# Far queries, far keys and four gate tiles by Strassen's scheme in a one-core decoder layer

## The chip, the core and the metric

The kernel runs on one NeuronCore of a Trainium2 chip. Five engines work side by side, each with its own instruction queue that is taken in order: PE (matrix multiply; its weight loads are shown as PEld), DVE (elementwise), ACT (elementwise and activation functions), POOL (here almost only an issuer of DMAs) and SP (an issuer of DMAs). Semaphores tie the queues together. The metric is the device time in microseconds: 840.95 us, the median of 3 runs (840.85 to 841.08).

## The reference

One decoder layer over 512 tokens of width 1024, in float32. All projections share one input, so they are one wide product `x @ w_in`:

```python
proj = x @ w_in[layer]
q = proj[..., :QKV_WIDTH]                      # 3 groups x 8 heads x 64; k and v likewise
u = proj[..., 3*QKV_WIDTH : 3*QKV_WIDTH+SSM_WIDTH]
gate_logits = proj[..., 3*QKV_WIDTH+SSM_WIDTH:]        # 2 x 1024
q, k = apply_rope(q, pos), apply_rope(k, pos)
for g, (window, dilation) in enumerate(((128, 1), (512, 4), (2048, 16))):
    o_g, lse_g = dilated_group_attention(q[:, :, g], k[:, :, g], v[:, :, g], window, dilation)
wts = softmax(stack(lses)); attn = sum(wts * outs)
y_attn = attn @ w_attn_br
y_s = s5_ssm(u, ...); glu = gelu(y_s) @ w_glu
y_ssm = (glu[..., :SSM_WIDTH] * sigmoid(glu[..., SSM_WIDTH:])) @ w_ssm_br
mixed = sigmoid(gates0) * y_attn + sigmoid(gates1) * y_ssm
h = layer_norm(alpha * x + mixed @ w_out)
x = layer_norm(alpha * h + (silu(h @ w_ff_gate) * (h @ w_ff_up)) @ w_ff_down)
```

Group 0 of the attention is called near, groups 1 and 2 together far.

## The kernel before

**Three products for one.** Each float32 operand is split into a rounded high part (a cast on ACT) and the rest (a subtraction on DVE); a product is then three matmuls, high by high, low by high, high by low (`mm3`, L202 to L204). A weight unit of 1 MB is loaded by SP into one of two `wraw` buffers, and its two halves are split into one of three slots (`whi`, `wlo`), in the order in which PE uses and releases them (class `Weights`).

**Steps.** The table `STEPS` at the top lists what PE does until the gated unit: 56 steps of 24 matmuls, each giving 128 output columns for all 512 tokens (or, for values, a quarter of the reduction for all heads). The order is: 4 steps of the state-space input u, 4 near values, 12 gates, 4 near keys, 4 near queries, then 12 steps of group 1 (values, keys, queries), 12 of group 2 and the last 4 gates. A key or query tile is multiplied by cosine and sine on DVE into a tile and a helper `z` (`qk_tile`); for each two tiles POOL adds the helper, rows shifted, into the tile with four accumulating DMAs (L769). A gate tile is finished by one ACT instruction into one of four gate buffers, which stay in SBUF until the branches use them.

**Work between the steps.** `fill` holds callables with a step number; half steps come after a step, whole ones in its middle. The attention works on pairs of heads, four near and four far: scores (PE), then on DVE a masked copy with the row maximum and on ACT the exponential, transposes of the weights (PE, copied by ACT), products with the values (PE). The tables `SCORES` and `WEIGHTS` say at which step each pair's scores and transposes stand. After step 56 come 4 steps of the gated unit, 8 of the two branch projections, 8 of the output projection, the first normalisation, and the feed-forward.

**A Strassen stage that is already there.** In the feed-forward, all but the first two pairs of output tiles are made by Strassen's scheme: seven products of 24 matmuls over 256 tokens in place of eight, with weight sums on DVE (`prepare`), the sums of the input made once, and the products joined on eviction (`product`, `evict`, L1303). That stage uses two extra slots and separate buffers for the weight sums.

Of the kernel before, what the change touches and what calls it, by code (L numbers as in the profile page):

```python
# [36 lines left out]
for _g, _order in ((1, "v0 v1 k0 k1 q0 q1"), (2, "k0 q0 v0 v1 k1 q1")):  # L37
    STEPS += [(o[0], _g, int(o[1]), _c) for o in _order.split() for _c in range(2)]
STEPS += [("g", 0, un, c) for un in range(6, 8) for c in range(2)]
# [9 lines left out]
SCORES = [[30, 33.5, 37, 40, 43.5], [44.5, 48.5, 52.5, 54, 55.5]]  # L49
WEIGHTS = [[32, 35.5, 38.5, 42], [46, 50, 53.5, 55]]  # L50
# [48 lines left out]
class Weights:  # L99


    def __init__(self, nc, pool, split):
        self.nc, self.split_to = nc, split
        self.units, self.raw, self.views = [], {}, {}
        self.free = deque((pool, n) for n in range(3))
        self.held = deque()
        self.pool = pool
        self.n_dma = self.n_split = 0
        self.first_job, self.jobs, self.first_loads, self.after = None, deque(), deque(), None
# [4 lines left out]
    def load(self):  # L114
# [3 lines left out]
        if self.first_loads and 2 * m == self.first_job:  # L118
            self.first_loads.popleft()()
            return  # L120
# [4 lines left out]
    def take_slot(self, n):  # L125
        pool, j = self.free.popleft()
        self.held.append((pool, j))
        hi = pool.tile([P, 1024], F32R, tag=f"whi{j}", name=f"whi{j}_{n}", bufs=1)
# [7 lines left out]
    def split(self):  # L136
# [3 lines left out]
        if self.jobs and n == self.first_job:  # L140
            self.jobs.popleft()()
            return
# [20 lines left out]
    def release(self):  # L163
        self.free.append(self.held.popleft())
# [3 lines left out]
def emit(ctx, tc, i, out):  # L168
# [71 lines left out]
    for n in range(2, N_GLU, 2):  # L240
# [5 lines left out]
        else:  # L246
            w.add(i["w_in"][2 + 6 * g + 2 * "kqv".index(kind) + un], 2 if kind == "v" else 8)
    for un in range(2):
# [9 lines left out]
    w.first_job = 2 * len(w.units)  # L258
# [480 lines left out]
    def turn_y():  # L739
        ysb = ssm["ysb"].rearrange("p a i b c -> p (a i) b c")  # L740
        yv = ydr.rearrange("(a x b h) (j c) -> x j h a b c", a=8, x=2, b=2, j=4)
        for x in range(2):
            for j in range(4):
                r0 = 64 * x + 16 * j
                for par in range(2):
                    sp.dma_start(yv[x][j][:, :, par], ysb[r0 : r0 + 16, :, par])
        ssm["ych"] = gat(2, "ych")
        sp.dma_start(ssm["ych"].rearrange("p (q t) -> p q t", q=4), ydr.rearrange("(q p) t -> p q t", p=P))
# [7 lines left out]
    def qk_tile(dv, ws, g, hp, name, mid):  # L756
        b = proj_tile(ws, f"p{name}{hp}", mid)
        if hp % 2 == 0:
            ssm["z"] = at.tile([P, 2, 512], F32, tag=("sw", "cq")[hp // 2], name=f"z{name}{hp}", bufs=1)
        z = ssm["z"]  # L760
        if g == 0:
            out, rot, args = as_phases(dv[:, hp, :]), as_phases(z[:, hp % 2, :]), [by_phase(v) for v in (b, rope[:, 0, :], rope[:, 1, :])]
        else:
            out, rot, args = dv[:, hp, :], z[:, hp % 2, :], (b, rope[:, 0, :], rope[:, 1, :])
        tt(out, args[0], args[1], ALU.mult)
        tt(rot, args[0], args[2], ALU.mult)
        if hp % 2 == 1:
            for q in range(4):
                pool.dma_start(dv[32 * q : 32 * q + 32, hp - 1 : hp + 1, :], z[32 * (q ^ 1) : 32 * (q ^ 1) + 32], accum_op=ALU.add)  # L769
# [19 lines left out]
    def attn_keys(kind, blk):  # L789
        if kind == 0:  # L790
            return [(qkv[0], kb) for kb in range(max(blk - 1, 0), blk + 1)]
        return [(qkv[1], blk), (qkv[2], blk)]

    def attn_scores(kind, hp):
        both = [(hh, slice(64 * hh, 64 * hh + 64)) for hh in range(2)]
        banks = {}
        for blk in range(NTT):
# [10 lines left out]
            for z, k0, nk, c in runs:  # L808
                for hh, rows in both:
                    pe.matmul(banks[hh][:, 256 * j + 128 * c : 256 * j + 128 * (c + nk)], z[0][rows, hp, qs],  # L810
                              z[1][rows, hp, 128 * k0 : 128 * (k0 + nk)], start=True, stop=True)
# [25 lines left out]
    def attn_values(kind, hp):  # L837
        ob = outs(f"o{kind}{hp}")
        for blk in range(NTT):
            ks, un = units.pop((kind, hp, blk))  # L840
            for c, (z, kb) in enumerate(ks):
                for hh in range(2):
                    h = 2 * hp + hh
                    pe.matmul(ob[64 * hh : 64 * hh + 64, 128 * blk : 128 * blk + 128],
                              z[2][:, kb, 64 * h : 64 * h + 64], un[:, hh, 128 * c : 128 * c + 128],
# [73 lines left out]
    gts = [None] * 4  # L919

# [633 lines left out]
```

## Time and profile before

| what | value |
|---|---|
| median of 3 runs | 840.95 us |
| the profiled execution | 841.21 us, of which the span of the core is 839.3 us |
| granted TensorE clock | 0.997 |
| busy: PE, PEld, DVE, ACT, POOL | 828.5, 724.0, 561.7, 357.3, 63.7 us |
| first far-stage step (step 28) | starts at 166.4 us |
| gated unit | starts at 371.6 us |
| Strassen products of the feed-forward | 515 to 712 us |

Busy time of PE is modelled with the drain of each matmul, so matmuls overlap in it: a matmul of 512 columns is shown as 0.39 us though the next one starts sooner. How much time a matmul takes on a full PE is therefore read from the distance between starts in the timeline, and the same holds for DVE and ACT. A wait is put down to the instruction that released it last.

### The profile page before, as it was taken

How to read it: one execution, taken by the hardware profiler on the slowest of the kernel's cores; microseconds unless marked ns; L12 is line 12 of the kernel's file. 1: busy time of each engine (PE TensorE's matmuls, PEld its weight loads, DVE VectorE, ACT ScalarE, POOL GpSimd, SP SyncE). 2: the span in 40 equal slices, each digit the busy share in tenths (PEclk: the TensorE clock that was granted, in tenths of full speed). 3: DMA queues.
4: the chain of work that ended last, by engine and by line, in shares of the span. 5: the costliest groups of instructions: out<-in, count | busy, mean ns of one | idle time of the engine just before them, and what ended most of it. 6: DMA issues, size and time to landing. Idle time of an engine off the chain costs nothing.

```text
span 839.3 us, 12913 instructions
## 1 busy us (share of the span) xinstructions
PE 828.5 (99%) x5296; PEld 724.0 (86%) x5296; DVE 561.7 (67%) x955; ACT 357.3 (43%) x541; POOL 63.7 (8%) x75
## 2 busy tenths in 40 slices
PE   9999999999999999999999999999999999999996
PEld 7888888888888788888888899999999999888885
DVE  7976899673444424345886698888888888533337
ACT  6863332255444344464233354444445545422211
POOL 0000001210213101100000420000000000000005
PEclk9999999999999999999999999999999999999998
DMA  9732423745545514312525143223333313722203
GB/s 337 191 107 102 125 101 84 182 99 186 103 126 96 134 51 111 92 51 101 229 82 191 51 164 138 102 101 104 112 114 118 107 51 101 293 85 86 88 1 101
DMA packets 27036, 100.66 MB, mean 120 GB/s; under 512 B 7136, under 2 KB 12000, under 8 KB 17376
## 3 DMA queue, kind: packets, MB, share of 16 engines
q1 hardware_dynamic: 23040, 91.83, 31.9%
q0 software_dynamic: 2304, 6.29, 5.8%
q10 hardware_dynamic: 1632, 1.70, 0.6%
q8 instruction: 42, 0.69, 0.3%
q14 instruction: 18, 0.15, 0.1%
HBM read 86.97 MB, written 6.55 MB: 111 GB/s over the span
## 4 chain that ended last, share of the span: by engine, by line
PE 93%; DVE 3%; DMA 2%; ACT 1%; issue 0%; POOL 0%; SPq 0%; DVEq 0%; ACTq 0%
PE dn L204 5%; PE dn L203 5%; PE dn L202 5%; PE pg L202 3%; PE pg L203 3%; PE pg L204 3%; PE pk L202 3%; PE pq L202 3%; PE pq L204 3%; PE pk L204 3%; PE pq L203 3%; PE pk L203 3%; PE pv L202 2%; PE pv L204 2%; PE pv L203 2%; PE pu L602 2%
## 5 line engine op out<-in xcount | busy, mean ns | idle before, releaser
L196 DVE TENSOR_TENSOR wlo<-raw,whi 128x1024 fp32r<-128x1024 f32 x94 | 115.0, 1226 | 121.7 <-ACT whi L195 121.4
L195 ACT CAST whi<-raw 128x1024 fp32r<-128x1024 f32 x94 | 98.3, 1049 | 164.0 <-PE dn L204 63.5
L1271 ACT CAST whi<-sums 128x1024 fp32r<-128x1024 f32 x40 | 42.0, 1050 | 95.9 <-DVE sums L337 95.9
L202 PE MATMUL dn<-whi,ffh 128*128 128x512 f32 x168 | 65.4, 389 | 0.0
L203 PE MATMUL dn<-wlo,ffh 128*128 128x512 f32 x168 | 65.4, 389 | 0.0
L204 PE MATMUL dn<-whi,ffl 128*128 128x512 f32 x168 | 65.4, 389 | 0.0
L202 PE MATMUL pg<-x_hi,whi 128*128 128x512 f32 x128 | 50.5, 395 | 0.0
L204 PE MATMUL pg<-x_hi,wlo 128*128 128x512 f32 x128 | 49.9, 390 | 0.0
L203 PE MATMUL pg<-x_lo,whi 128*128 128x512 f32 x128 | 49.9, 390 | 0.0
L337 DVE TENSOR_TENSOR wlo<-sums,whi 128x1024 fp32r<-128x1024 f32 x40 | 48.7, 1220 | 0.0
L202 PE MATMUL pq<-x_hi,whi 128*128 128x512 f32 x96 | 37.9, 394 | 0.0
L202 PE MATMUL pk<-x_hi,whi 128*128 128x512 f32 x96 | 37.8, 394 | 0.0
L769 POOL DMA_DIRECT2D k<-zk x24 | 19.0, 1212 | 246.0 <-DMA raw<-in_w_in 137.9
L204 PE MATMUL pq<-x_hi,wlo 128*128 128x512 f32 x96 | 37.4, 390 | 0.0
L204 PE MATMUL pk<-x_hi,wlo 128*128 128x512 f32 x96 | 37.4, 389 | 0.0
L203 PE MATMUL pk<-x_lo,whi 128*128 128x512 f32 x96 | 37.4, 389 | 0.0
L203 PE MATMUL pq<-x_lo,whi 128*128 128x512 f32 x96 | 37.4, 389 | 0.0
L203 PEld LDWEIGHTS dn<-wlo,ffh 128*128 128x128 f32 x168 | 31.5, 188 | 6.6
L202 PEld LDWEIGHTS dn<-whi,ffh 128*128 128x128 f32 x168 | 31.5, 188 | 6.5
L204 PEld LDWEIGHTS dn<-whi,ffl 128*128 128x128 f32 x168 | 31.5, 188 | 6.5
L823 ACT ACTIVATE un<-un,st 128x256 f32<-128x256 f32 (+1 forms) x64 | 30.8, 483 | 8.7 <-DVE st L821 8.7
L337 DVE TENSOR_TENSOR q<-pq,rope 128x512 f32<-128x512 f32 x12 | 9.9, 827 | 35.8 <-PE pq L204 35.8
(654 smaller groups left out, 2375.6 us busy)
## 6 DMA issues: line engine op xcount, KB each, us to landing
raw<-in_w_in SPq DMA_DIRECT2D x26, 1024.0 KB, 4.9
raw<-in_w_dn SPq DMA_DIRECT2D x11, 1024.0 KB, 4.8
ra<-in_w_gu SPq DMA_DIRECT2D x10, 1024.0 KB, 4.8
rb<-in_w_gu SPq DMA_DIRECT2D x10, 1024.0 KB, 4.9
raw<-in_w_br SPq DMA_DIRECT2D x4, 1024.0 KB, 4.8
raw<-in_w_out SPq DMA_DIRECT2D x4, 1024.0 KB, 4.8
k<-zk POOLq DMA_DIRECT2D x24, 128.0 KB, 4.3
q<-zq POOLq DMA_DIRECT2D x24, 128.0 KB, 4.1
```

The costliest lines, as they stand in the source:

```text
L195: act.copy(hi, src)
L196: dve.tensor_tensor(lo, src, hi.bitcast(F32), op=ALU.subtract)
L202: pe.matmul(dst, a[0], b[0], start=first, stop=False)
L203: pe.matmul(dst, a[0], b[1], start=False, stop=False)
L204: pe.matmul(dst, a[1], b[0], start=False, stop=last)
L337: eng.tensor_tensor(o, a, b, op=op)
L602: pe.matmul(bs[e][:, cs], wk[a], xk[b], start=(k + a + b + cs.start == 0), stop=(k == KT - 1 and a == 1))
L769: pool.dma_start(dv[32 * q : 32 * q + 32, hp - 1 : hp + 1, :], z[32 * (q ^ 1) : 32 * (q ^ 1) + 32], accum_op=ALU.add)
L823: act.activation(pt, pt, AF.Exp, bias=mneg, scale=-1.0, accum_out=zsum)
L1271: act.copy(hi, src)
```

## The change

The 24 steps of groups 1 and 2 and the last 4 gates become 8 steps of values (both far groups) and five "quads". A quad is two 256-column weight blocks side by side, 512 output columns: for the first four, the keys and queries of two head pairs of one far group; for the last, the four last gate tiles. Each quad is seven products of 24 matmuls over 256 tokens (`quad_product`), in the order 1, 5, 6, 2, 7, 3, 4; its weights are prepared in the order 1, 5, 6, 2, 4, 7, 3 (`prepare_quad`), the sums written over the loaded weights, and the next quad's weights loaded by quarters of 512 KB as each quarter comes free. A fourth slot is lent by attention buffers (`X_HOMES`).

The input x is read a second time from DRAM in float32 (`fetch_x`, two POOL DMAs of 1 MB), its sums are made in place on DVE and split in steps 32 to 35. The twelve early gate tiles are stored to DRAM as they are finished and read back after the quads (`park_gates`, `fetch_gates`, POOL); the reading back of the state-space output moves from SP, right behind its stores, to POOL, behind the last quad's DMAs (`fetch_y`). The far scores and most near ones move to later places, between the products; the gated unit cycles through three banks instead of four; the merging of the two attention halves moves about 1.5 steps later. Keys and queries of two head pairs now share a tile, and four accumulating DMAs complete one pair. Step numbers keep their scale: the quads take 36 to 56, four steps each.

```diff
+STEPS += [("v", _g, _un, _c) for _g in (1, 2) for _un in range(2) for _c in range(2)]
+QUADS = [(1, 0), (1, 1), (2, 0), (2, 1), (None, 3)]
...
-SCORES = [[30, 33.5, 37, 40, 43.5], [44.5, 48.5, 52.5, 54, 55.5]]
-WEIGHTS = [[32, 35.5, 38.5, 42], [46, 50, 53.5, 55]]
+SCORES = [[30, 36.3, 39.1, 41.9, 44.7], [49.5, 52.5, 54, 55.7, 58.2]]
+WEIGHTS = [[32, 38.1, 40.9, 43.7], [51, 53.2, 55, 57.2]]
...
     def release(self):
-        self.free.append(self.held.popleft())
+        slot = self.held.popleft()
+        if slot[0] is None and not self.extra_ok():
+            return
+        self.free.append(slot)
         self.split()
...
+    def fetch_x():
+        for n, h in enumerate(("g0", 2)):
+            forms_x[n] = home(h, f"xf{n}").rearrange("p (k t) -> p k t", k=KT)
+            pool.dma_start(forms_x[n], i["xk"][n].rearrange("p (k t) -> p k t", k=KT))
...
+    at_step(30.6, fetch_x)
+    for n in range(4):
+        at_step(32 + 0.4 * n, sums_x, n)
+        at_step(33 + 0.4 * n, split_x, n)
...
+    QORDER, QPREP = (1, 5, 6, 2, 7, 3, 4), (1, 5, 6, 2, 4, 7, 3)
+    def prepare_quad(j, n):
+        if n in (5, 6, 4):
+            w.flush()
...
+        if n == 5:
+            tt(a21, a21, a22, ALU.add)
+        elif n == 6:
+            tt(a21, a21, a11, ALU.subtract)
+            load_quad(j + 1, 0)
+        elif n == 4:
+            tt(a12, a12, a21, ALU.subtract)
+            tt(a21, a22, a21, ALU.subtract)
+        src = {1: a11, 5: a21, 6: a21, 2: a12, 7: a21, 3: a12, 4: a22}[n]
+        act.copy(hi, src)
+        w.flush()
+        def rest():
+            tt(lo, src, hi.bitcast(F32), ALU.subtract)
+            if n in (7, 3, 4):
+                load_quad(j + 1, {7: 2, 3: 1, 4: 3}[n])
+        w.after = rest
...
+    def quad_product(j, n):
...
+        for e in range(2):
+            for k in range(4):
+                for m, (p_, q_) in enumerate(((wh, mh), (wh, ml), (wl, mh))):
+                    pe.matmul(d[:, 256 * e : 256 * e + 256], p_[:, e, k, :], q_[:, k, :], ...)
...
+    def quad_out(j, f, h, src):
...
+        tt(dst[:, :, cs], src, c, ALU.mult)
+        tt(z[:, :, cs], src, r, ALU.mult)
+        if (f, h) in ((0, 1), (1, 0)):
+            turn_half(dst, z)
...
+        if n in (1, 5, 6):
+            act.copy(s[n], z if n == 5 else x)
+        elif n == 2:
+            tt(s[1], s[1], y, ALU.add)
+            quad_out(j, 0, 0, s[1])
+        elif n == 7:
+            tt(s[5], s[5], x, ALU.add)
+            quad_out(j, 1, 1, s[5])
+        elif n == 3:
+            tt(s[6], s[6], z, ALU.add)
+            quad_out(j, 0, 1, s[6])
+        else:
+            quad_out(j, 1, 0, x)
```

How the rows move on DVE. First the kernel before, in the middle of the far keys and queries (`wlo` are weight splits, `pk` and `pq` the PE results):

```order
L337 TENSOR_TENSOR k_1925<-pk_2100,rope 128x512
L337 TENSOR_TENSOR zk_2091<-pk_2100,rope 128x512
L196 TENSOR_TENSOR wlo_38_2132<-raw_1980,whi_38_2131 128x1024
L337 TENSOR_TENSOR q_2157<-pq_2158,rope 128x512
L337 TENSOR_TENSOR zq_2183<-pq_2158,rope 128x512
L196 TENSOR_TENSOR wlo_39_2187<-raw_1980,whi_39_2186 128x1024
```

And the change, in the third quad and the first preparations of the fourth (`rq` are the loaded weights, `qy`, `qx`, `qz` the three PE banks of a quad, `qsnap` saved products, `kq` the tile of keys and queries, `qz_2908` and `qz_2940` the helpers with the sine part):

```order
L345 TENSOR_TENSOR qsnap<-qsnap,qy_2881 128x512
L345 TENSOR_TENSOR kq_2907<-qsnap,rope 128x2x256
L345 TENSOR_TENSOR qz_2908<-qsnap,rope 128x2x256
L345 TENSOR_TENSOR wlo_q_2879<-rq_1893,whi_q_2878 128x1024
L345 TENSOR_TENSOR qsnap<-qsnap,qx_2770 128x512
L345 TENSOR_TENSOR kq_2907<-qsnap,rope 128x2x256
L345 TENSOR_TENSOR qz_2940<-qsnap,rope 128x2x256
L345 TENSOR_TENSOR wx_q_2911<-rq_1893,wx_q_2911 128x1024
L345 TENSOR_TENSOR rq_1987<-rq_1987 128x1024
L345 TENSOR_TENSOR wlo_q_2945<-rq_1987,whi_q_2944 128x1024
L345 TENSOR_TENSOR qsnap<-qsnap,qz_2806 128x512
L345 TENSOR_TENSOR kq_2907<-qsnap,rope 128x2x256
```

Three instructions for each tile of 128 columns are now 22 for each quad of 512, and a weight sum (`rq_1987<-rq_1987`) stands directly ahead of the split of the same sum (`wlo_q_2945`).

On POOL, before, between the near queries and the far ones:

```order
L769 DMA q_1468<-zq_1494 32x1024 x4
L769 DMA q_1468<-zq_1563 32x1024 x4
L769 DMA k_1925<-zk_1973 32x1024 x4
L769 DMA k_1925<-zk_2091 32x1024 x4
L769 DMA q_2157<-zq_2183 32x1024 x4
```

And the change, from the near queries to the end of the quads:

```order
L768 DMA kq_1428<-zq_1567 32x2x512 x4
L1068 DMA xf_1909<-in_xk 128x2048
L1068 DMA xf_1911<-in_xk 128x2048
L768 DMA kq_2265<-qz_2266 32x1024 x4
L768 DMA kq_2265<-qz_2321 32x1024 x4
L768 DMA kq_2587<-qz_2588 32x1024 x4
L768 DMA kq_2587<-qz_2670 32x1024 x4
L882 MEMSET wt 128x4x96
L768 DMA kq_2907<-qz_2908 32x1024 x4
L768 DMA kq_2907<-qz_2940 32x1024 x4
L768 DMA kq_3180<-qz_3181 32x1024 x4
L768 DMA kq_3180<-qz_3212 32x1024 x4
```

The two reads of x now stand between the near queries and the first quad. Behind the last row follow the read of `ych` (which SP issued before) and the three reads of the gates.

On PE, the first far scores before, behind the first step of group 2's values (`pv`):

```order
L203 MATMUL pv_2599<-wlo_44_2481,x_hi_93 128x512
L204 MATMUL pv_2599<-whi_44_2480,x_lo_95 128x512
L810 MATMUL s_2630<-k_1925,q_2157 128x128
L810 MATMUL s_2631<-k_1925,q_2157 128x128
L810 MATMUL s_2630<-k_2366,q_2484 128x128
```

And in the change, inside the fourth quad, right behind its third product:

```order
L1151 MATMUL qx_3020<-x23h,wlo_q_2982 128x256
L830 MATMUL s_3114<-kq_2265 128x128
L830 MATMUL s_3115<-kq_2265 128x128
L830 MATMUL s_3114<-kq_2907 128x128
L830 MATMUL s_3115<-kq_2907 128x128
```

They read the first head pair's half of `kq_2907`, the tile that the third quad has just written. The third quad's last but one product completes that half: its join (`qsnap<-qsnap,qz_2806`), two multiplications and four accumulating DMAs follow it; the second pair's half is completed by the last product. Before, a whole step of values stood between the last tile that the scores read and the scores.

249 lines of the change are left out of this document (183 added, 66 removed).

## The prediction

> **What bounds the kernel now.** I read the page's busy table first, then PE's waits, then the stretches.
>
> ```profile
> span 839.3 us, 12913 instructions
> PE 828.5 (99%) x5296; PEld 724.0 (86%) x5296; DVE 561.7 (67%) x955; ACT 357.3 (43%) x541; POOL 63.7 (8%) x75
> PE fs10x L1303 <- DVE quad L337: 0.8, 1, 0.8
> PE s L810 <- DMA q<-zq: 0.5, 1, 0.5
> 220.00:371.60 151.60, 150.99 (x978) 125.76 (x976) 62.60 (x158) 69.50 (x166) 22.43 (x29) 1.00 0.41 102
> 516.00:700.00 184.00, 184.00 (x1536) 184.00 (x1535) 157.54 (x149) 91.78 (x110) 0.00 (x0) 1.00 0.28 98
> ```
>
> PE never rests: in the stretch that the quads replace (220 to 371.6) it is busy for 150.99 of 151.60 us, and its longest waits are below a microsecond. So time changes by what PE has to issue, and by whatever makes it wait anew. The last row is the stage that already works by Strassen's scheme: PE is full, its weight loads are full too (184.00 of 184.00), and DVE is busy for 86%, against 41% in the stretch of the quads today. The change turns one kind of stretch into the other, so I ask what PE saves, and whether DVE can follow.
>
> **PE's saving.** A matmul's cost is the distance between starts.
>
> ```profile
> 229.74 0.39 PE L203 MATMUL pq<-x_lo,whi 128*128 128x512 f32 x1
> ...
> 232.69 0.39 PE L204 MATMUL pq<-x_hi,wlo 128*128 128x512 f32 x1
> ```
>
> ```profile
> 526.63 2.88 PE fs2x L1303 x24
> ```
>
> 512 columns: 13 distances in 2.95 us, 0.2269 each. 256 columns: a product of 24 takes 2.88, 0.120 each; that is more than half of 0.2269, so the eighth that the scheme saves is not all kept. Four steps of 24 take 96 x 0.2269 = 21.78; a quad takes 7 x 2.88 = 20.16. Saved: 1.62 a quad, **8.1 for five**. The values, and the matmuls of the attention, are the same in number. The Trainium skill, "TensorE: Matmul & The Clock Gate", section "Back-to-back issue gap", gives columns / 2.4 plus 2.5 ns for a single warm matmul, 109.2 and 215.8 ns; by that the five quads would save 11.9, but this trace does not agree (0.120 and 0.2269), since its weight loads are as full as PE.
>
> **DVE's work in a quad.** Prices from the stage that has the same operations:
>
> ```profile
> 604.50 0.69 DVE L337 TENSOR_TENSOR quad<-snap,fs5z 128x512 f32<-128x512 f32 x1 [1.64 <-PE fs5z L1303]
> 605.10 1.22 DVE L337 TENSOR_TENSOR wlo<-rb,whi 128x1024 fp32r<-128x1024 f32 x1
> 607.30 0.69 DVE L337 TENSOR_TENSOR quad<-snap,fs5x 128x512 f32<-128x512 f32 x1 [0.99 <-PE fs5x L1303]
> 607.91 1.22 DVE L337 TENSOR_TENSOR sums<-rb 128x1024 f32<-128x1024 f32 x1
> 609.04 1.22 DVE L337 TENSOR_TENSOR wlo<-ra,whi 128x1024 fp32r<-128x1024 f32 x1
> 610.18 1.22 DVE L337 TENSOR_TENSOR sums<-sums,ra 128x1024 f32<-128x1024 f32 x1
> ```
>
> ```profile
> 609.24 1.05 ACT L1271 CAST whi<-sums 128x1024 fp32r<-128x1024 f32 x1 [5.22 <-DVE sums L337]
> ```
>
> From start to start 1.14 for 128x1024 and 0.61 for 128x512. A key and query quad has 4 sums and 7 splits (11 x 1.14 = 12.54), 3 joins and 8 rope products (11 x 0.61 = 6.71): 19.25. Where a split stands directly behind its sum, DVE waits for the sum's drain, the hand-over and the cast, about 1.22 + 0.15 + 1.05 after the sum began, so 1.28 after its own next start; this happens once a quad, and two shorter ones make it 1.5. Together **20.75 of DVE against 20.16 of PE**. The rope operand is broadcast over two tiles; the near rope, with its phase layout, is the upper bound (1.09), the far one the lower (0.69):
>
> ```profile
> 150.31 1.09 DVE L337 TENSOR_TENSOR q<-pq,rope 128x512 f32<-128x512 f32 x1 [0.72 <-PE pq L204]
> 244.91 0.69 DVE L337 TENSOR_TENSOR q<-pq,rope 128x512 f32<-128x512 f32 x1 [2.83 <-PE pq L204]
> ```
>
> I take the lower: the quad's operand runs through contiguous 256-element pieces. The upper adds 8 x 0.4 = 3.2 a quad.
>
> What lets DVE follow is the attention between the products, PE time in which no weights are needed:
>
> ```profile
> 233.07 1.68 PE o L844 x28
> 234.75 1.72 PE s L810 x16
> ...
> 244.87 1.53 PE t L833 x14
> ```
>
> ```profile
> 355.24 1.90 PE o L844 x32
> 357.14 1.99 PE s L810 x32
> 364.80 1.75 PE t L833 x16
> ```
>
> ```profile
> 343.99 0.42 DVE L821 CUSTOM_DVE_ANT_0 un<-s,masks 128x256 f32<-128x256 f32 x1 [0.52 <-PE s L810]
> ...
> 346.41 0.42 DVE L821 CUSTOM_DVE_ANT_0 un<-s,masks 128x256 f32<-128x256 f32 x1
> ```
>
> `o` are the value pieces, `s` the scores, `t` the transposes. The quads hold: first, scores, values, transposes, values, scores (28.5); second, transposes, values, scores (25.1); third, transposes and values (23.4); fourth, far scores and transposes (23.9); PE 100.9 in all. DVE: 4 x 20.75 and four sets of scores (eight operations, 2.42 + 0.35 = 2.8; the near ones have two shorter among them): 94.2. The fifth quad has gates, finished on ACT: 11 x 1.14 + 3 x 0.61 + 2 x 2.8 = 20.0, well below its 31.4 (20.16 and two far scores, values and transposes each). So DVE has 6.7 us to spare over four quads, but in the third and fourth it is nearly level with PE, and there I look for waits.
>
> **The far scores' wait.** They stand behind three products of the fourth quad, 8.64 after its start T, and read the pair that the third quad's last but one product completes. DVE from that quad's second join on (product 2 ends at T - 8.64, 0.2 to hand over): join and two rope products 1.83, split 1.14, join and two 1.83, split 1.14, sum 1.14, the 1.28, split 1.14, join and first rope product 1.22: the last rope product starts at T + 2.3. From such a start to the scores, before:
>
> ```profile
> 335.76 0.69 DVE zq L337
> ...
> 336.74 1.50 POOL q L769 x2
> 338.23 4.87 DMA q<-zq
> 343.24 1.80 PE s L810 x26
> ```
>
> 7.48. So they can go on at T + 9.8 and PE is there at 8.64 plus 0.1 for the two matmuls that read another tile: **about 1.0 of waiting**. Two splits in the third and fourth quads come 0.1 and 0.2 late by the same addition: **0.3**. Bounds: 0, and rival A below.
>
> **The second reading of x.** POOL's two reads wait in order behind SP's stores out of the buffer they fill:
>
> ```profile
> 185.78 9.14 SPq L746 DMA_DIRECT2D ydr<-ysb  x16
> 196.84 0.39 SPq L748 DMA_DIRECT2D ych<-ydr  x1
> ...
> 199.13 1.53 PE t L833 x14
> ```
>
> ```profile
> raw<-in_w_in SPq DMA_DIRECT2D x26, 1024.0 KB, 4.9
> xn<-in_x SPq DMA_DIRECT2D x2, 1024.0 KB, 7.8
> hdr<-hn SPq DMA_DIRECT2D x4, 512.0 KB, 12.8
> raw_x<-in_xw SPq DMA_DIRECT2D x3, 512.0 KB, 5.3
> ```
>
> Landed at 196.84 + 1.2 of issue + 4.9, 7.8 or 12.8: 203, 206 or 211. I take 206, as two transfers go together. The first quad starts where the transposes at 199.13 and three and a half steps of 24 x 0.2269 have passed: 199.13 + 1.53 + 2.72 + 3 x 5.45 = 219.7. Behind x, which all later DVE work in order waits for, stand 18 operations of 1.14 (x's four sums and four splits, and the weights' sums and splits up to there) and some 2.5 for casts: 23, so DVE is free at 229, 9.5 after the first quad's start, for the second near scores; their exponentials, 348.38 + 0.19 - 343.99 = 4.6 from the first of them as far ones, are done by 14.1, and the transposes are due behind four products and two pieces, 4 x 2.88 + 3.40 = 14.9: margin 0.8, price nothing; at 211 it is 5 - 0.8, so 4 us.
>
> ```profile
> 348.38 0.19 ACT L823 ACTIVATION_READ_ACCUMULATOR un<-un,st 128x1 f32 x1
> ```
>
> **The rest moves at no price.** POOL stands idle until its first accumulation, so storing the gates delays nothing; their return (3 MB, and 1 MB of the state-space output) has the gated unit's four steps, 21.8 us, as cover, and would cost at most one landing of 12.8 if it had none. The loads by quarters need 5.3 for 512 KB and have at least three products and the attention, 10. The merges move by 1.5 steps into the branch steps; three banks leave the gated unit two tiles ahead of its eviction. Without that cover each would hold PE for about one of its tiles' steps, 2.7 us.
>
> **Sum**, against the profiled execution (841.2, 0.26 above the median): 841.2 - 8.1 + 1.0 + 0.3 = 834.4, as a median **834.2**.
>
> **Rivals.**
>
> *Some of the waits are larger* (A). Either x lands late (834.2 + 4 = 838), or no DVE operation can start before the one ahead is drained: 11 x 1.22 + 11 x 0.69 + 1.5 = 22.5 a quad, scores 8 x 0.5 = 4.0, so 4 x 22.5 + 4 x 4.0 = 106 against 100.9, 5.2 of waiting in place of 1.3 and **about 838**. Against it: the rows at 609.04 and 610.18 start 1.14 apart though each is 1.22 long. The Trainium skill, "VectorE: DVE Perf Modes", section "The DRAIN you can't avoid", says that the next operation doesn't start until the pipe is empty; these rows do not agree.
>
> *DVE sets the pace* (B), slower than before. The one mechanism: in its fixed order DVE stands at joins whose product isn't done, and cannot make up for it since splits queue behind them. In the existing stage such waits are 1.64 and 0.99 within six microseconds (rows at 604.50 above and 607.30 in the same list). If each quad has those, 2.8 with hand-over, at undrained prices 22.5 + 2.8 = 25.3, and scores at 4.0: 4 x 29.3 = 117.2 against 100.9, 16.3 of waiting in place of 1.3, **849**. It decides from 100.9 + 8.1 on, that is above 27.2 of DVE per quad with its scores; my sum has 23.6. For it: joins, sums and splits are chained through buffers that are reused in place. Against: in 516 to 700 the same waits cost PE nothing.
>
> *The accumulating DMAs starve on POOL* (C), a second, rarer way to be slower: DVE is far busier while POOL must issue. Issue at four times its length (13.4 in place of 3.34) makes the far scores 10 later, 844. Against it:
>
> ```profile
> 100.00:150.00 50.00, 50.00 (x222) 41.40 (x221) 47.56 (x73) 12.36 (x14) 4.51 (x7) 1.00 0.38 116
> 138.72 3.34 POOL L769 DMA_DIRECT2D k<-zk  x4 [137.86 <-DMA raw<-in_w_in]
> ```
>
> With DVE busy for 47.56 of 50 us four issues took 3.34, 0.84 each, hardly more than the two in 1.50 at 336.74, 0.75 each.
>
> *The change does not do what it says* (D): 256-column matmuls in this stretch cost 0.13 or more. At 21.78 / 168 = 0.1296 nothing is saved and with the waits it is 841 to 842.3, no change. Against it: 0.120 at full weight loads over 184 us.
>
> **How the numbers follow.** Forecast (832.3 to 836) 0.60, A 0.14, B 0.12, C 0.04, D 0.06, and 0.04 for several small covers gone, near 840. A measurement of this kernel can tell about 0.2%, 1.7 us: faster is below 839.3, slower above 842.6. Faster: 0.60 + 0.14 = 0.74. Same: D's 0.06, the 0.04, and the low end of B, 0.02: 0.12. Slower: 0.10 of B and C's 0.04, 0.14. The range: low end 832.3, no new wait at all and the old 0.46 before the far scores gone (841.2 - 8.1 - 0.5 - 0.3 = 832.3); high end 839.3, which takes in A and leaves the dearer cases out.
>
> **What would show it.** Each product in the quads at 2.88; between first quad and gated unit PE waits of 1 to 2 us in all, the largest at the far scores on the accumulating DMA; DVE 85 to 95% busy in the third and fourth quads, with splits and sums 1.14 apart; x landing before 207 and no wait at the second near transposes. Wrong: product lengths above 3.0 (D), PE waiting for `wlo` splits over and over (A, B), accumulations issued in more than 4 us (C), or a wait at the transposes of the first quad.

## The result and the profile after

The changed kernel takes 835.55 us, the median of 4 runs (835.03 to 835.75); the kernel before, beside it, 840.92 (840.85 to 841.08). The ratio is 0.9935, with a 95% interval of 0.9918 to 0.9952: faster by 0.65%, 5.4 us. The forecast was 834.2, in a range of 832.3 to 839.3. The profiled execution took 835.37.

The page of the changed kernel, and PE's waits in it (waited for: us in total, times, longest):

```profile
span 833.6 us, 13772 instructions
PE 822.0 (99%) x5656; PEld 736.3 (88%) x5656; DVE 621.1 (75%) x1013; ACT 381.9 (46%) x579; POOL 70.2 (8%) x84
PE qx L1151 <- ACT qsnap L1184: 0.7, 1, 0.7
PE s L830 <- DMA kq<-qz: 0.4, 1, 0.4
```

PE is still the bound, busy for 99%. The list of waits names little more than one microsecond that is new, but it leaves out what is hidden in short stretches, such as matmuls that start late one by one. The accounts below are therefore made from starts of matmuls. They use three marks: the first matmul of the far values, the first of the first quad, and the first of the down projection. From the first to the last mark the kernel before takes 711.82 - 166.43 = 545.39, the changed one 705.30 - 166.48 = 538.82: **6.57 less**. Behind the last mark the change loses 0.8 again (below). A whole span also contains the start of the kernel, where the first mark moved between 165.79 and 166.67 in the runs of this study; the distances between marks leave that out.

The products run as forecast. Two pieces of the chain of work that ended last (start, length, count):

```profile
229.41 2.88 PE qx L1151 x24
232.29 2.88 PE qy L1151 x24
```

The five quads by engine (us; busy time and instructions of PE, PEld, DVE, ACT, POOL; granted clock, DMA share, GB/s):

```profile
219.81:249.13 29.32, 29.32 (x270) 27.54 (x271) 24.19 (x39) 16.28 (x35) 2.48 (x4) 1.00 0.26 77
249.13:274.56 25.43, 25.43 (x229) 24.62 (x229) 22.88 (x53) 18.20 (x48) 3.83 (x5) 1.00 0.52 120
274.56:298.48 23.92, 23.79 (x213) 23.28 (x211) 18.03 (x20) 10.81 (x15) 6.72 (x9) 1.00 0.61 135
298.48:324.40 25.92, 24.77 (x218) 24.12 (x217) 25.42 (x42) 12.43 (x26) 6.76 (x9) 1.00 0.54 123
324.40:357.04 32.64, 32.56 (x330) 30.77 (x329) 21.18 (x50) 24.07 (x59) 7.75 (x11) 1.00 0.70 194
```

In the first three quads PE has hardly any idle time by this table, which does not show matmuls that start a tenth late. In the fourth it is busy for 24.77 of 25.92, and there DVE is busy for 25.42: it is the one place where DVE looks like the pace. In the third, DVE has 18.03 of 23.92. Its timeline from the third quad into the fourth shows why the two did not even out (start, length, operation, idle time before it and what ended it):

```profile
289.65 0.69 DVE L345 TENSOR_TENSOR qsnap<-qsnap,qy 128x512 f32<-128x512 f32 x1 [4.49 <-PE qy L1151]
...
295.78 1.22 DVE L345 TENSOR_TENSOR rq<-rq 128x1024 f32<-128x1024 f32 x1
298.19 1.23 DVE L345 TENSOR_TENSOR wlo_q<-rq,whi_q 128x1024 fp32r<-128x1024 f32 x1 [1.19 <-ACT whi_q L1122]
...
300.66 0.68 DVE L345 TENSOR_TENSOR qz<-qsnap,rope 128x512 f32<-128x512 f32 x1
```

DVE has run out of work at 285.2 and stands for 4.49 us, since the next operation joins a product that PE has not finished, and the weights behind it have no free slot. Then it works from 289.65 on nearly without a pause, but for the 1.19 in which it waits for the cast of a sum that it has only just made. The last product with the sine that the far scores need starts at 300.66, 2.18 behind the fourth quad's start of 298.48.

PE and ACT in the fourth quad (the same columns):

```profile
305.12 0.39 PE L1151 MATMUL qx<-x23h,whi_q 128*128 128x256 f32 x1 [0.72 <-ACT qsnap L1184]
...
308.18 0.71 PE L830 MATMUL s<-kq 64*128 64x128 f32 x6
309.31 0.38 PE L830 MATMUL s<-kq 64*128 64x128 f32 x2 [0.42 <-DMA kq<-qz]
```

```profile
302.59 2.00 ACT L1122 CAST whi_q<-rq 128x1024 fp32r<-128x1024 f32 x2 [4.43 <-DVE rq L345]
304.50 0.57 ACT L1184 COPY qsnap<-qx 128x512 f32<-128x512 f32 x1
```

The third product of the quad is due at 304.24 and starts at 305.12, 0.88 late. It writes the bank of the first product, and the copy that empties that bank stands in ACT's queue behind two casts, of which the first waited 4.43 for DVE. Then the far scores (32 matmuls) take 2.89, from 308.18 to 311.07, where undisturbed ones take 1.98: 0.9 of waiting. The kernel before had the same delay there, 2.90 from 286.12 to 289.02, and 2.58 at the second far pair, from 342.38 to 344.96.

### The profile page after: what moved, and what is told of

The parts are those of the page before. It is cut to its first block, busy times and chain, and to the rows that moved or that the text cites. A ratio compares the mean times of both kernels' runs of the same rounds, so it can differ in the third digit from the quotient of the medians.

```text
span 833.6 us, 13772 instructions
## 1 busy us (share of the span) xinstructions
PE 822.0 (99%) x5656; PEld 736.3 (88%) x5656; DVE 621.1 (75%) x1013; ACT 381.9 (46%) x579; POOL 70.2 (8%) x84
## 4 chain that ended last, share of the span: by engine, by line
PE 68%; DVE 4%; DMA 2%; ACT 1%; issue 1%; POOL 0%; DVEq 0%; ACTq 0%
PE qx L1151 5%; PE dn L209 5%; PE dn L210 5%; PE dn L211 5%; PE qz L1151 2%; PE qy L1151 2%; PE wo L209 2%; PE wo L210 2%; PE b L210 2%; PE wo L211 2%; PE b L209 2%; PE b L211 2%; PE o L864 2%; PE fs9x L1498 1%; PE fs8x L1498 1%; PE fs7x L1498 1%
## 5 line engine op out<-in xcount | busy, mean ns | idle before, releaser
L203 DVE TENSOR_TENSOR wlo<-raw,whi 128x1024 fp32r<-128x1024 f32 x74 | 90.8, 1230 | 93.3 <-ACT whi L202 93.3
L202 ACT CAST whi<-raw 128x1024 fp32r<-128x1024 f32 x74 | 77.3, 1049 | 105.3 <-PE dn L211 63.5
L1122 ACT CAST whi_q<-rq 128x1024 fp32r<-128x1024 f32 x28 | 29.2, 1052 | 41.8 <-DVE rq L345 41.8
L345 DVE TENSOR_TENSOR wlo_q<-rq,whi_q 128x1024 fp32r<-128x1024 f32 x28 | 34.1, 1222 | 12.9 <-ACT whi_q L1122 12.6
L209 PE MATMUL pg<-x_hi,whi 128*128 128x512 f32 x96 | 37.6, 392 | 0.0
L210 PE MATMUL pg<-x_lo,whi 128*128 128x512 f32 x96 | 37.4, 389 | 0.0
L768 POOL DMA_DIRECT2D kq<-qz x32 | 25.2, 1313 | 108.7 <-PE s L830 48.2
L345 DVE TENSOR_TENSOR wlo<-ra,whi 128x1024 fp32r<-128x1024 f32 x20 | 24.4, 1222 | 1.8 <-ACT whi L1466 1.8
L209 PE MATMUL pv<-whi,x_hi 128*128 128x512 f32 x64 | 25.4, 396 | 0.0
L210 PE MATMUL pv<-wlo,x_hi 128*128 128x512 f32 x64 | 25.0, 390 | 0.0
```

The costliest lines, as they stand in the source:

```text
L202: act.copy(hi, src)
L203: dve.tensor_tensor(lo, src, hi.bitcast(F32), op=ALU.subtract)
L209: pe.matmul(dst, a[0], b[0], start=first, stop=False)
L210: pe.matmul(dst, a[0], b[1], start=False, stop=False)
L345: eng.tensor_tensor(o, a, b, op=op)
L768: pool.dma_start(dst[32 * q : 32 * q + 32], z[32 * (q ^ 1) : 32 * (q ^ 1) + 32], accum_op=ALU.add)
```

## The experiments

All distances in this table end at the first matmul of the down projection; the differences are against the changed kernel. The last column starts at the first matmul of the third quad's first product (276.00 in the changed kernel, a distance of 429.30). Each edited kernel was profiled once.

| run | from the first far value | difference | from the first quad | difference | from the third quad, difference |
|---|---|---|---|---|---|
| the change | 538.82 | | 485.49 | | |
| `e_copy` | 538.39 | -0.43 | 485.27 | -0.22 | +0.29 |
| `e_far` | 538.12 | -0.70 | 485.00 | -0.49 | +0.15 |
| `e_copyfar` | 538.63 | -0.19 | 485.51 | +0.02 | +0.15 |
| `e_turn` | 538.63 | -0.19 | 485.49 | 0.00 | 0.00 |
| `e_dve_early` | 538.33 | -0.49 | 485.21 | -0.28 | +0.35 |
| `e_dve_late` | 541.08 | +2.26 | 487.95 | +2.46 | +3.10 |
| `e_sine` | 536.50 | -2.32 | 483.38 | -2.11 | -1.87 |
| `e_pe` | 550.39 | +11.57 | 496.80 | +11.31 | +6.09 |
| `e_merge` | 537.22 | -1.60 | 484.10 | -1.39 | -0.79 |
| `e_pool` | 540.89 | +2.07 | 487.77 | +2.28 | +1.82 |
| `e_x` | 544.89 | +6.07 | 486.92 | +1.43 | +0.13 |
| `e_best` | 536.85 | -1.97 | 483.73 | -1.76 | -1.13 |

The first column of differences holds 0.2 that the changed kernel's profiled execution lost right ahead of its first quad and nearly all other runs did not. The second holds something more. The first two quads together, which most of the edits do not touch, take 56.20 in the changed kernel and in `e_turn`, 56.06 in `e_copyfar`, 55.69 in `e_copy`, and 55.56 to 55.59 in `e_far`, `e_dve_early`, `e_dve_late`, `e_merge` and `e_best`. They follow the moment at which DVE begins with x: 38.99 and 38.80 behind the first far value, then 38.65, 38.27 and 37.86 to 38.19. So the changed kernel's profiled execution has 0.6 of small waits in its first two quads that go with a late x (that x is their cause was not tested by itself), and an edit that acts behind them must not be credited with their absence. For such edits the last column is the one to read. In it the landing of the accumulating DMAs ahead of the first far scores still moves by 0.4 from run to run: from the last product with the sine to the scores it took 8.65 in the changed kernel, 8.66 in `e_turn`, 8.82 in `e_x`, 8.94 in `e_copy` and 9.06 in `e_dve_early`, though that product started 2.18 or 2.19 behind the fourth quad's start each time. Differences below 0.4 are therefore not told apart from none.

### Two waits, each taken away

The first edit lets the changed kernel prepare one set of weights a product later, behind the eviction copy:

```diff
             quad_evict(j, n)
+            if (j, m) == (3, 0):
+                w.held.appendleft(qslot.pop((2, 4)))
+                w.release()
+            if (j, n) == (2, 4):
+                continue
             w.held.appendleft(qslot.pop((j, n)))
             w.release()
```

> Edit: the weights that are prepared when the third quad's last product is done are prepared one product later, so that ACT's copy of the fourth quad's first product (the eviction that frees bank x) stands ahead of one of the two casts that it stands behind now. Measured by the starts of PE's matmuls; the first matmul of the down projection is at 705.30 in the changed kernel. Theory 1 (ACT's queue holds the bank: the copy comes 0.88 late because two casts stand ahead, and the far scores right behind it are held by the accumulating DMA anyway until 309.3): the wait of 0.88 at the third product falls below 0.2, the wait at the far scores grows by as much, the down projection starts within 0.2 of 705.3. Theory 2 (the prediction's: the split of the product's own weights comes late): the wait stays at about 0.9. Theory 3 (both waits count in full): the wait falls and the down projection starts 0.9 earlier.

The wait at the bank went (ACT's queue had held it), and in its place PE waited 0.44 in the same product for the weight split, and 1.1 in place of 0.4 at the far scores. Behind the second quad nothing was gained (+0.29, as much as the accumulation landed later). So theory 3 falls, and theory 1 holds in kind: the bank's wait was ACT's queue, and the scores are held by the DMA anyway. Its wait below 0.2 was not reached, since theory 2's split stands close behind.

The second edit moves the far scores by one product and their transposes by one:

```diff
-SCORES = [[30, 36.3, 39.1, 41.9, 44.7], [49.5, 52.5, 54, 55.7, 58.2]]
-WEIGHTS = [[32, 38.1, 40.9, 43.7], [51, 53.2, 55, 57.2]]
+SCORES = [[30, 36.3, 39.1, 41.9, 44.7], [50.2, 52.5, 54, 55.7, 58.2]]
+WEIGHTS = [[32, 38.1, 40.9, 43.7], [51.9, 53.2, 55, 57.2]]
```

> Edit: the first far scores stand behind the fourth product of the fourth quad instead of behind the third, their transposes behind the fourth quad instead of its last but one product. Theory 1 (the scores wait for the DMA, 0.9 with the matmuls between): that wait is gone, the 0.88 at the third product stays, the down projection starts about 0.9 earlier, at 704.4. Rival (the wait is only handed on, to the transposes or to the splits that DVE does later since it has the score copies later): the down projection starts within 0.3 of 705.3.

PE's largest waits in that run:

```profile
PE o L864 <- ACT un L855: 1.6, 1, 1.6
...
PE qx L1151 <- ACT qsnap L1184: 0.7, 1, 0.7
```

The wait at the scores is gone, and a new one of 1.6 stands at the far values, whose transposed weights ACT copies late, behind casts that wait for DVE's sums. The wait of 0.9 that was taken away has come back whole: behind the second quad the run is 0.15 longer, which is the rival's outcome. The -0.49 from the first quad lies ahead of the edit.

> Both edits: the eviction copy ahead of one cast, and the far scores one product later. Theory 1: both waits gone, 0.9 and 0.88, so the down projection starts about 1.8 earlier, at 703.5, though the first edit alone gives nothing. Rival (DVE sets the pace of the third and fourth quads): another wait, for a weight split, takes their place and less than 1 is gained.

Both edits together: no gain at all (+0.15 behind the second quad). The far values wait 1.6, the third product 0.4, a later one 0.35 for a join. This is the rival's outcome: a wait that is removed in the fourth quad comes back at the next place, because, as the next runs show, the work behind it on DVE ends no earlier. The first theory, of two independent waits, fell here.

> Edit: of the third quad's two sets of four accumulating DMAs, which POOL issues back to back, the second set (the pair that is not wanted yet) is issued behind the far scores. Theory 1 (the second set lengthens the first one's way: 7.3 us from POOL's start to the scores, where the kernel before had 6.5): the way falls to about 6.5, the wait at the far scores vanishes (PE gets there at 308.2), the down projection starts 0.4 to 0.9 earlier. Rival (the way is set by other traffic, the loads by quarters): it stays at 7.3 and nothing moves.

```diff
-        if (f, h) in ((0, 1), (1, 0)):
+        if (j, f, h) == (2, 1, 0):
+            at_step(49.7, turn_half, dst, z)
+        elif (f, h) in ((0, 1), (1, 0)):
             turn_half(dst, z)
```

Nothing moved, but the edit did not do what it was to do either. POOL has nothing between the two sets, so it issued them back to back as before:

```profile
301.94 6.32 POOL L768 DMA_DIRECT2D kq<-qz  x8 [20.22 <-PE qx L1151]
```

Whether the second set lengthens the first one's way is left open by it. What the stretches of the changed kernel show is other traffic in the same microseconds: in 304 to 306 the DMA engines are busy for 0.91 at 264 GB/s, in 306 to 308 fully, since SP starts a quarter load of the next quad's weights at 302.55; at the corresponding accumulations of the kernel before (336.7 to 338.7) they were busy for 0.37 at 43 GB/s.

```profile
304.00:306.00 2.00, 1.28 (x11) 1.07 (x10) 2.00 (x2) 2.00 (x4) 2.00 (x6) 1.00 0.91 264
306.00:308.00 2.00, 2.00 (x19) 2.00 (x18) 1.93 (x3) 0.50 (x2) 2.00 (x3) 1.00 1.14 201
```

```profile
336.70:338.70 2.00, 2.00 (x11) 1.65 (x10) 2.00 (x3) 0.00 (x0) 1.96 (x4) 1.00 0.37 43
```

That the loads are the cause fits and was not tested by itself.

### Does DVE set the pace, and where?

More DVE work ahead of its pause in the third quad, and as much behind it:

```diff
-            tt(lo, src, hi.bitcast(F32), ALU.subtract)
+            for _ in range(2 if (j, n) in ((2, 4), (2, 7)) else 1):
+                tt(lo, src, hi.bitcast(F32), ALU.subtract)
```

> Edit: two weight splits of the third quad (its products 4 and 7), which DVE makes right ahead of a pause of 4.5 us in that quad, are made twice: 2 x 1.14 = 2.3 us more DVE. All runs are read from the first matmul of the far values (166.48 in the changed kernel) to the first of the down projection (705.30): 538.8; before 545.4. Theory (DVE has slack in the first three quads that it cannot carry on, since there are only four slots): within 0.3 of 538.8. Rival (DVE is the bound in all quads): 541.

In `e_dve_late` the pairs are (3, 1) and (3, 5).

> Edit: two weight splits of the fourth quad (its products 1 and 5), which DVE makes behind that pause, are made twice: again 2.3 us more DVE. Theory (from the end of the third quad to the end of the fourth DVE works without pause and sets the pace, so that what is removed at one wait comes back at the next): the distance grows by 1.8 to 2.5, to 540.6 to 541.3. Rival (the waits are the queues' and the DMAs' own, each by itself): 0.5 to 1 more at most.

2.3 us more ahead of the pause cost DVE nothing: the pause shrinks to 2.09, and the last product with the sine starts 2.18 behind the fourth quad's start, as in the changed kernel. The +0.35 in the last column is the accumulation, which landed 0.4 later.

2.3 us more behind the pause came back at PE as 2.5 of waiting: the fourth quad's second product, on time in the changed kernel, starts 1.32 late, and its third 2.01 late in place of 0.88. PE's two longest waits in the quads of that run:

```profile
PE qx L1152 <- ACT qsnap L1185: 1.8, 1, 1.8
PE qz L1152 <- DVE qsnap L345: 1.2, 1, 1.2
```

The whole run lost more, 3.10 behind the second quad, because the clock fell behind these waits (told at the end): the third product then took 1.5 longer, in part in place of the wait at the far scores. The scores could have gone on 13.35 behind the quad's start (the sine at 4.70 and a way of 8.65), and PE came there at 13.72, so by this estimate the clock made at most 0.4 of the 3.10 and DVE's work the rest. So from 289.65 to the far scores in the fourth quad DVE is the path, nearly microsecond for microsecond, and in the third quad ahead of that it is not.

Less DVE work:

```diff
-        tt(z[:, :, cs], src, r, ALU.mult)
+        if j == 0:
+            tt(z[:, :, cs], src, r, ALU.mult)
```

> Edit: left out are the products with the sine in quads 2 to 4 (the first quad's helper is added in their place), so 4 x 0.61 = 2.4 us less DVE in each. Theory (DVE sets the pace of the fourth quad): the waits of 0.3, 0.9 and 0.9 in it and those at the far transposes behind it vanish nearly all, the distance falls by 1.5 to 2.5, to 536.3 to 537.3. Rival (ACT's order and the accumulating DMAs): it falls by less than 0.7.

1.87 less behind the second quad (2.1 to 2.3 from the earlier marks), as forecast. No wait of over 0.12 is left in any product; only the far scores still wait, 0.8, for their DMA.

More PE work:

```diff
+        for _ in range(2 if n == 5 else 1):
             for e in range(2):
```

> Edit: in each of the five quads product 5 is made twice, 5 x 2.88 = 14.4 us more PE. Theory (PE is the bound but for some 2 to 3 us in the fourth and fifth quads, which are DVE's): the added products cover those waits, the distance grows by 12 to 13, to 551 to 552. Rival A (PE alone is the bound, waits are those of single transfers and stay): 14.4, to 553.2. Rival B (DVE sets the pace of all quads): clearly less than 12.

11.3 to 11.6 of 14.4, just under the theory's 12 to 13: the longer products cover some 3.0 us of waits. For 2.88 each, the five quads (each from its first product to the next quad's) grew by 2.44, 2.78, 2.88, 1.01 and 2.21, so 1.9 of the covered waits lie in the fourth quad and 0.7 in the fifth, as the theory had it, and 0.5 in the first two, which it did not have. The third takes the added product whole; a wait of 0.28 in it stays. This sizes what the change loses inside the quads: **about 3 us**.

### The cheapest microsecond

> Edit: one merging step of the near pairs moves ahead by one product (46.5 to 46.28). It has no costly work of its own, but in front of it the pending weight split is written out; so the split that stands directly behind its sum in the third quad (and makes DVE wait 1.19 for the cast) now stands behind the next join and its two products. Read from the first quad's first matmul to the first of the down projection, 485.5 in the changed kernel. Theory (DVE sets the pace of the fourth quad): the third quad's last products with cosine and sine start about 1.2 earlier, the waits at the third product and at the far scores shrink by 1.2 in all, the distance falls by 0.8 to 1.2, to 484.3 to 484.7. Rival (another wait of DVE takes its place): less than 0.3.

```diff
-    at_step(46.5, merge_near, 1)
+    at_step(46.28, merge_near, 1)
```

1.39 less by the forecast's measure, a little over the range; but 0.6 of that lies in the first two quads, ahead of the edit. Behind them it is 0.79, the low end of the range. DVE in that run, at the place shown above:

```profile
294.97 1.22 DVE L345 TENSOR_TENSOR rq<-rq 128x1024 f32<-128x1024 f32 x1
296.10 0.68 DVE L345 TENSOR_TENSOR qsnap<-qsnap,qz 128x512 f32<-128x512 f32 x1
296.82 0.69 DVE L345 TENSOR_TENSOR kq<-qsnap,rope 128x512 f32<-128x512 f32 x1
297.43 0.68 DVE L345 TENSOR_TENSOR qz<-qsnap,rope 128x512 f32<-128x512 f32 x1
298.03 1.22 DVE L345 TENSOR_TENSOR wlo_q<-rq,whi_q 128x1024 fp32r<-128x1024 f32 x1
```

Between the sum and its split there is now a join with two products, and the pause of 1.19 for the cast is gone; the third product of the fourth quad is on time. The last product with the sine starts at 297.43, against the fourth quad's start 2.4 earlier than in the changed kernel, though the scores could go on only at 307.75: the accumulation's way was 10.3 here, 8.65 in the changed kernel (300.66 to 309.31) and 7.48 before.

### Work moved to POOL

```diff
-        tt(z[:, :, cs], src, r, ALU.mult)
+        tt(z[:, :, cs], src, r, ALU.mult, eng=pool if f == h else dve)
```

> Edit: two of the four products with the sine of each quad, those whose accumulation isn't due yet, are made by POOL in place of DVE; nothing is left out. DVE has 1.2 us less in each quad, POOL 2 x about 1.3 more. Theory: the distance falls by half of what leaving out all four gave (2.1), so 0.8 to 1.2, to 484.3 to 484.7. Rival (POOL reads SBUF while DVE works and one holds the other up): DVE operations beside POOL's take longer than 1.22 and 0.69, and the distance falls by less than 0.4 or grows.

2.3 **more** (1.8 behind the second quad): the rival. POOL and DVE at the start of that stretch:

```profile
290.26 1.80 POOL L345 TENSOR_TENSOR qz<-qsnap,rope 128x512 f32<-128x512 f32 x1 [7.46 <-DVE qsnap L345]
293.81 1.80 POOL L345 TENSOR_TENSOR qz<-qsnap,rope 128x512 f32<-128x512 f32 x1 [1.75 <-DVE qsnap L345]
```

```profile
290.82 2.32 DVE L345 TENSOR_TENSOR wlo_q<-rq,whi_q 128x1024 fp32r<-128x1024 f32 x1
...
294.38 2.32 DVE L345 TENSOR_TENSOR wx_q<-rq,wx_q 128x1024 fp32r<-128x1024 f32 x1
```

A DVE operation of 128x1024 that meets one of POOL's takes 2.32 in place of 1.22. So DVE gives up 0.61 and pays 1.1. The Trainium skill, "SBUF — State Buffer", section "SBUF: two separate sides", says that a DVE operation with two inputs from SBUF and a GpSimd one that reads SBUF shut each other out for a whole instruction; the trace agrees in kind, and its price here is 1.1 of an overlap of 1.2.

### x a transfer later

```diff
             forms_x[n] = home(h, f"xf{n}").rearrange("p (k t) -> p k t", k=KT)
+            if n == 0:
+                pool.dma_start(forms_x[n], i["xk"][1].rearrange("p (k t) -> p k t", k=KT))
```

> Edit: POOL reads 1 MB more into the first of x's two buffers ahead of x, so that x itself lands later by one transfer. In the changed kernel x lands at 205.3 and the transposes of the second near pair are on time. Theory (margin of 0.8, then microsecond for microsecond): if x lands 5 later PE waits about 4 in the first quad and the distance from the first far value matmul to the first of the down projection grows by 3 to 4.5, to 542 to 543.3. Rival (the first quad has more slack than was worked out): under 1.

DVE's first sum of x came 4.64 later (measured from the first far value matmul), and the distance grew by 6.07, more than the 3 to 4.5 of the theory. The first quad started 4.64 later: there is no margin. It is not the transposes that come first, but the first product itself:

```profile
PE qx L1153 <- ACT v L802: 4.7, 1, 4.7
```

ACT's queue, in the changed kernel, holds the copy of the last value tile, whose bank the quad needs, behind two casts that wait for x's sums:

```profile
217.28 1.05 ACT L1122 CAST whi_q<-rq 128x1024 fp32r<-128x1024 f32 x1 [3.69 <-DVE rq L345]
218.23 1.04 ACT L202 CAST x_hi<-xf 128x1024 fp32r<-128x1024 f32 x1
219.18 2.04 ACT L802 COPY v<-pv 128x512 f32<-128x512 f32 x4
```

The quad starts at 219.81, 0.2 behind the last value matmul's due end. The remaining 1.4 of the 6.07 is 1.8 by the clock, which is told at the end, less the small waits of the first two quads, of which this run has 0.5 less.

### A better version

`e_merge` and the later far scores, with the transposes left where they are:

```diff
-SCORES = [[30, 36.3, 39.1, 41.9, 44.7], [49.5, 52.5, 54, 55.7, 58.2]]
+SCORES = [[30, 36.3, 39.1, 41.9, 44.7], [50.2, 52.5, 54, 55.7, 58.2]]
-    at_step(46.5, merge_near, 1)
+    at_step(46.28, merge_near, 1)
```

> Edit: the merging step one product earlier, as in the run that gained 1.4 in the stretch, and the first far scores behind the fourth product of the fourth quad instead of the third, their transposes left where they are. Theory: the wait of 0.7 (0.9 with the matmuls between) at the far scores, which the first edit alone left, goes, since PE gets there 2.88 later; the transposes are 5.8 behind the scores and the exponentials take 4.6, so they are on time; from the first quad's first matmul to the down projection 483.2 to 483.7 (485.5 in the changed kernel, 484.1 with the first edit alone), the median 833.2 to 834.0. Rival (the DVE and ACT work behind the scores hands the wait on to the far values, as in the run that moved scores and transposes): 484.0 to 484.6, the median 834 to 834.6.

833.5 us, the median of 5 runs (832.88 to 834.15), beside 840.76 for the kernel before: a ratio of 0.9915 (0.9901 to 0.9928). The stretch came out at 483.73, between the two theories: the wait at the scores (0.9) is gone, and 0.7 of waiting has come up at the far values (`PE o L864 <- ACT un L855: 0.7, 1, 0.7`). The changed kernel's ratio lies at 0.9935 (0.9918 to 0.9952), so the times alone do not part the two for certain; the stretch does, by 1.13 behind the second quad (the 1.76 from the first quad holds 0.6 that lies ahead of both edits).

## Why the prediction was right, point by point

**The saving of PE (8.1): right.** Products take 2.88, as in the feed-forward stage. With the 3.0 us of waits covered, the changed kernel is 6.57 + 3.0 = 9.6 ahead of the kernel before: 8.1 from the matmuls and 1.5 from two old waits of the far scores (0.92 and 0.60 above the 1.98 of an undisturbed set), of which the sum counted none and the range's low end only 0.46. The waits view had named no more than that. The prediction gave full weight loads as the reason why 512 columns take 0.2269; its rows show them full for 256 columns alone (in 220 to 371.6 they are busy for 125.76 of PE's 150.99), so that reason stays open. The sum does not rest on it.

**DVE's prices: right.** Starts are 1.14 and 0.61 apart, and the broadcast rope operand costs 0.6 (290.38 to 290.98 in the third quad), so the lower of the two bounds was the one to take. The pause between a sum and its own split is 1.19 (1.28 in the sum). Rival A's drain did not show.

**Nearly level in the third and fourth quads: half right.** The fourth is, the third is not: it had 4.5 us to spare that DVE could not carry over. The sum of the quad's work did not show this; the order of instructions does, with four slots and a join ahead.

**The far scores' wait (1.0): right in size (0.9), by two errors that cancel.** The last product with the sine starts at T + 2.2, where T + 2.3 was worked out. But the accumulation took 8.65 to the scores in place of 7.48, and PE came 1.1 later than the 8.64 that was assumed. That the two agree is luck.

**Two late splits (0.3): mis-sized, and the mechanism incomplete.** The split in the third quad cost 0.28, where 0.1 was forecast. The fourth quad's third product came 0.88 late and not 0.2, by ACT's queue: the copy that frees a bank stands behind casts that wait for DVE. The prediction worked out when DVE's results come and never when ACT's do. The same cause stands at the far transposes and values behind it (0.45 at 337.30, and 0.2 to 0.3 at the values). Waits in all: about 3, where 1.3 were forecast.

**The second reading of x: the times right, the margin wrong.** x landed at 205.3 (206 forecast), the first quad started at 219.81 (219.7). The margin of 0.8 at the transposes was of no account, since the first product itself was just on time, held by ACT's queue once more. The price was not quite nothing: 0.6 of small waits in the first two quads go with a late x.

**The rest moved at no price: right, as far as the profile shows.** PE's list of waits names none between the quads and the end of the feed-forward that the kernel before does not have too.

**The rivals.** A forecast 838 by waits of 4 to 5; there were 3. B (849) would need DVE to set the pace in all quads; in `e_pe` the first three took 2.44, 2.78 and 2.88 of an added 2.88, and in `e_dve_early` the third had 2.3 to spare, which excludes it, though in the fourth quad its mechanism is at work. C: POOL issues accumulations 0.79 apart (eight in 6.32) with DVE full, and 0.75 apart (two in 1.50) with DVE idle in the kernel before. D: 2.88.

**The sum.** -8.1 - 1.5 + 3.0 = -6.6 against the forecast -6.8 on PE. That these lie so close is luck in part: a gain of 1.5 and 1.7 of waiting, neither of them counted, cancel. There is also a loss at the end of the kernel that was not forecast: from the first matmul of the down projection to the end of the span the kernel before takes 127.5, the changed one 128.3, and all twelve edited kernels within 0.1 of that. PE, DVE and the last issue of a DMA keep their distances (829.64 is 6.51 less than 836.15); the 0.8 lies behind that issue (3.9 to the end, before 3.2). The last packet of the output lands 1.67 behind it in both kernels, so the loss lies in the closing instructions of the program: SP's last one and POOL's next stand 0.17 apart before and 0.84 in the change. What holds POOL there stays open. With it the profiled execution is 5.84 faster, of 6.8 forecast.

## What to carry to other kernels

Where a scheme trades matmuls for elementwise work, compare engine against engine not by the quad but by the stretch between two points at which the in-order queues must meet: a spare 4.5 us in one quad did nothing for the next, where DVE was the path. There, a removed wait comes back at the next place, and the lever is the engine's own work and its self-made pauses: putting a join between a weight sum and the split of that sum gained 0.8 us for one changed number. When single runs are compared, start the measure behind everything that the edit cannot touch: here 0.6 of what looked like a gain went with the arrival of x. When the time of a bank is worked out, follow the queue of the engine that empties it too: two casts that wait for another engine ahead of a copy were the largest new wait here.

## What the runs showed of the hardware that was not expected

**The clock falls with waits of 2 to 5 us.** In `e_x` PE stood still for 4.7 us ahead of the first quad. Stretches of that run (the granted clock is the third number from the end):

```profile
219.00:223.80 4.80, 0.17 (x1) 0.00 (x0) 2.61 (x3) 2.47 (x4) 0.00 (x0) 0.73 0.01 2
223.80:228.00 4.20, 4.14 (x19) 4.14 (x20) 3.14 (x3) 2.40 (x5) 0.00 (x0) 0.50 0.00 0
228.00:236.00 8.00, 8.00 (x83) 7.27 (x82) 7.79 (x18) 4.67 (x12) 0.00 (x0) 1.00 0.30 94
```

For the next 4.2 us the clock was 0.50 and the matmuls stood 0.21 apart in place of 0.12; the first product took 4.89 (223.86 to 228.75) in place of 3.06. So a wait of 4.7 cost 1.8 more. In `e_dve_late` no wait was longer than 2.0 and the clock fell all the same, 1 us after PE had gone on:

```profile
301.70:304.50 2.80, 2.80 (x23) 2.80 (x24) 2.80 (x4) 0.37 (x1) 0.99 (x2) 1.00 0.03 6
304.50:306.66 2.16, 0.31 (x4) 0.11 (x2) 2.16 (x4) 2.16 (x4) 2.16 (x5) 1.00 0.88 154
307.70:311.10 3.40, 3.40 (x18) 3.33 (x16) 3.37 (x3) 1.26 (x2) 2.13 (x3) 0.50 1.09 181
```

A single wait of 1.8 in `e_far` (1.6 in the list of waits) was not followed by a fall. The Trainium skill, "TensorE: Matmul & The Clock Gate", section "Part 1: The HAM clock gate", gives half the clock after an idle window of about 3.4 us and until as long a one has been busy; `e_x` agrees, with 4.7 idle and 4.2 of work until the full clock, and `e_dve_late` does not, since PE was never idle for that long. How much idle time in what stretch it takes is not shown by these runs.

**POOL's arithmetic nearly doubles a DVE operation of 128x1024 beside it**, 2.32 in place of 1.22, while POOL's DMA issues did not slow it: those of the changed kernel run beside splits of 1.22 to 1.23.
